# Two of a unit's four weight-block sums as accumulating transfers, and raw blocks loaded one by one

## The chip, the cores and the metric

The kernel runs on one core of one Trainium2 chip. The metric is device time in microseconds (us); a run's time is a little longer than the profile's span, which goes from the first to the last instruction. The engines are TensorE (PE: matmuls; PEld: its weight loads), VectorE (DVE), ScalarE (ACT), GpSimd (POOL) and SyncE (SP). SP and GpSimd issue nearly all DMA transfers, each in the order of its own queue.

## The reference

One layer of a hybrid decoder on 1024 prompt tokens and 8 decode tokens:

```
hn = rmsnorm(x, g_norm)
u  = hn @ w_in                       # 1024 -> 7176 columns
xa, za, q, k, v, o, zb, i, f = split(u)
yA = RG-LRU(conv(xa))                # a linear recurrence over the tokens
yB = rmsnorm(sigmoid(o) * mLSTM(q, k, v, i, f))
x  = x + concat[yA * silu(za), yB * silu(zb)] @ w_out
y  = rmsnorm(x, g_final)
```

The change lies in `hn @ w_in`, the input projection of the prompt tokens.

## The kernel before, in words

The wide columns of `w_in` are done in 14 units (`UNITS`, L44), each of two groups of 256 columns, such as `x0y0` (256 columns of xa, 256 of za). Unit 0 is done with plain products while the activations are read. Units 1 to 13 use Winograd's form of Strassen's scheme: a unit's weights are four blocks of 512 x 256, `blk(u, a, b)` with a the column group and b the half of the contraction (written A00, A01, A10, A11 for ab), the activations are cut in halves likewise, and seven products P1, P2, P5, P6, P7, P3, P4, in that order, stand in for eight. Fourteen operands of the activations (`cb`, high and low parts for seven products) are made once, in `x_combos` (L465).

Products are taken to fp32 accuracy by splitting each operand into a rounded high part and a low part (`split`, L70: ScalarE casts to `wh` on L72, VectorE subtracts to `wl` on L73) and three matmuls (`mm3`, L64, lines 66 to 68).

`prep(u, q)` (L276) makes the weight operand of product q. It forms four sums in place on VectorE, each over 128 x 1024 elements (L279, L280, L282, L288):

```
P5:  A00 = A00 - A10        L279
     A10 = A10 + A11        L280
P6:  A10 = A11 - A00        L282
     A01 = A01 - A10        L288, behind P6's split
```

and then splits A00 for P1, A01 for P2, A10 for P5, A10 for P6, A00 for P7, A01 for P3, A11 for P4. At P5, ahead of the sums, `dec_unit` (L251) multiplies all four raw blocks with the 8 decode tokens (L257). Raw blocks come from `w_in` through SP, 512 KB each (`load_raw`, L234 to L244), into two tiles: `raw0` with A00 and A10, `raw1` with A01 and A11. Both blocks of `raw0` are loaded for the next unit behind P7's split, both of `raw1` behind P4's.

`product(u, q)` (L299) runs the two halves s = 0 and 1 of a product, 24 matmuls of 512 columns in all (in v and o units 48 of 256). P1, P6, P7 and P4 add up in one accumulator (`ps_kv`), P2, P5 and P3 in another (`ps_o`), and `evac` (L325) takes a copy or a sum after each: ScalarE copies after P1, P5, P6 (L328, L335, L338) and P4 (L353), VectorE adds after P2, P7, P3 (L331, L341, L345). P6's copy on L338 must be done before P7 adds to the same accumulator. Outputs are stored by GpSimd's queue (`stq`).

The order of work is written out: the loop over `seq` (L1688) calls `preps`, which runs `LEAD` = 2 products ahead, then the product, and `pop_bg` after each half, which slips in one step of other work: gates, the RG-LRU (L772 are gate activations, L820 the gate products, L866 to L877 its stores), the decode step of the mLSTM (L988 to L1009). Each engine keeps its instructions in the order that the build lays out. Split operands live in six buffers (`NWS`, three products). The mLSTM over the prompt, the output projection and the final norm come after the units.

Of the kernel before, what the change touches and what calls it, by code (L numbers as in the profile page):

```python
# [17 lines left out]
P = 128  # L18
# [4 lines left out]
NH = 4  # L23
# [28 lines left out]
def hymba_kernel(  # L52
# [11 lines left out]
    def mm3(out, ah, al, bh, bl, first, last):  # L64

        TE.matmul(out, ah, bh, start=first, stop=False, skip_group_check=True)  # L66
        TE.matmul(out, ah, bl, start=False, stop=False, skip_group_check=True)  # L67
        TE.matmul(out, al, bh, start=False, stop=last, skip_group_check=True)  # L68

    def split(hi, lo, src):  # L70

        a = A.copy(hi, src)  # L72
        V.tensor_tensor(lo, src, hi.bitcast(F32), op=ALU.subtract)  # L73
        return a
# [7 lines left out]
    def ps(tag, shape):  # L82
        return psp.tile(shape, F32, tag=tag, name=f"ps_{tag}", bufs=NBUF.get(tag, 1))
# [139 lines left out]
    def run_late():  # L223
        now = late[:]
        late.clear()
        for f in now:
            f()
# [6 lines left out]
    def load_raw(u, b, parts=(0, 1)):  # L234

        if u >= len(units):
            return
        if (u, b) not in raws:
            raws[u, b] = rawp.tile([P, 4, 512], F32, tag=f"raw{b}", name=f"raw{b}_{u}")
        for a in parts:  # L240
            kind, j = units[u][a]
            c = COL[kind] + j * 256
            ld(raws[u, b][:, :, a * 256:(a + 1) * 256],
               w_in[0, b * HT:(b + 1) * HT, c:c + 256].rearrange("(k p) c -> p k c", p=P))  # L244
# [28 lines left out]
    def blk(u, a, b):  # L273
        return raws[u, b][:, :, a * 256:(a + 1) * 256]

    def prep(u, q):  # L276
        if q == Q_P5:
            dec_unit(u)
            V.tensor_tensor(blk(u, 0, 0), blk(u, 0, 0), blk(u, 1, 0), op=ALU.subtract)  # L279
            V.tensor_tensor(blk(u, 1, 0), blk(u, 1, 0), blk(u, 1, 1), op=ALU.add)  # L280
        if q == Q_P6:
            V.tensor_tensor(blk(u, 1, 0), blk(u, 1, 1), blk(u, 0, 0), op=ALU.subtract)  # L282
        src = {Q_P1: (0, 0), Q_P2: (0, 1), Q_P5: (1, 0), Q_P6: (1, 0), Q_P7: (0, 0), Q_P3: (0, 1), Q_P4: (1, 1)}
        hi, lo = ws([P, 4, 256], f"wh{u}_{q}"), ws([P, 4, 256], f"wl{u}_{q}")
        split(hi, lo, blk(u, *src[q]))
        wops[u, q] = hi, lo
        if q == Q_P6:
            V.tensor_tensor(blk(u, 0, 1), blk(u, 0, 1), blk(u, 1, 0), op=ALU.subtract)  # L288
        b = {Q_P7: 0, Q_P4: 1}.get(q)
        if b is not None:  # L290
            if u + 1 < len(units):
                load_raw(u + 1, b)
            else:
                if b == 1:
                    r_open(0)

    px = {}

    def product(u, q):  # L299

        kind = units[u][0][0]
        wh, wl = wops.pop((u, q))
        bh, bl = cb[q]
        first, last = q in (Q_P1, Q_P2, Q_P5), q in (Q_P2, Q_P3, Q_P4)
        for s in range(2):
            if q == Q_P1:
                px["X", s] = ps("kv", [P, 512])
            if q in (Q_P2, Q_P5):
                px["Y", s] = ps("o", [P, 512])
            X, Y = px["X", s], px.get(("Y", s))  # L310
            out = X if q in (Q_P1, Q_P6, Q_P7, Q_P4) else Y
            if kind in "vo":
                for i in range(2):
                    t = slice((2 * s + i) * P, (2 * s + i + 1) * P)
                    for k in range(4):
                        mm3(out[:, i * 256:(i + 1) * 256], bh[:, k, t], bl[:, k, t], wh[:, k, :], wl[:, k, :],
                            first and i == 0 and k == 0, last and i == 1 and k == 3)
            else:
                c = slice(s * P, (s + 1) * P)
                for k in range(4):  # L320
                    mm3(out, wh[:, k, c], wl[:, k, c], bh[:, k, :], bl[:, k, :], first and k == 0, last and k == 3)
            evac(u, q, s, X, Y)
            yield

    def evac(u, q, s, X, Y):  # L325
        if q == Q_P1:
            px["s1", s] = t = sg([P, 512], "s1")
            A.copy(t, X)  # L328
        elif q == Q_P2:
            t = px.pop(("s1", s))  # L330
            V.tensor_tensor(t, t, Y, op=ALU.add)  # L331
            emit_out(u, 0, 0, s, t)
        elif q == Q_P5:
            px["s5", s] = t = sg([P, 512], "s5")
            A.copy(t, Y)  # L335
        elif q == Q_P6:
            px["s2", s] = t = sg([P, 512], "s2")
            A.copy(t, X)  # L338
        elif q == Q_P7:
            t = px.pop(("s5", s))  # L340
            V.tensor_tensor(t, t, X, op=ALU.add)  # L341
            emit_out(u, 1, 1, s, t)
        elif q == Q_P3:
            t = px.pop(("s2", s))
            V.tensor_tensor(t, t, Y, op=ALU.add)  # L345
            emit_out(u, 0, 1, s, t)
        else:
            t = sg([P, 512], "c21")
            o = units[u][1][0] == "o"
            if o:  # L350
                A.activation(t, X, AF.Tanh, scale=0.5)
            else:
                A.copy(t, X)  # L353
            emit_out(u, 1, 0, s, t, o)

    def silu2(t):
# [108 lines left out]
    def x_combos(i):  # L465

        p0, p1 = xps[i]
        s = slice(i % 4 * P, (i % 4 + 1) * P)
        f0, f1 = bf["f"]

        def out(q, t):
            split(cb[q][0][:, :, s], cb[q][1][:, :, s], t)
        if i >= 4:
            t3 = sg([P, 4, P], "t3")
            V.tensor_tensor(t3, f1, f0, op=ALU.subtract)
            out(Q_P7, t3)
        else:
            t1, t2, t4 = (sg([P, 4, P], f"t{n}") for n in (1, 2, 4))
            V.tensor_tensor(t1, f0, p0, op=ALU.subtract)
            V.tensor_tensor(t2, f1, t1, op=ALU.subtract)  # L480
            V.tensor_tensor(t4, p1, t2, op=ALU.subtract)
            out(Q_P6, t2)
            out(Q_P5, t1)
            out(Q_P4, t4)
# [1191 lines left out]
    last_u = len(units) - 1  # L1676
    unit_of = {p: u for u, pair in enumerate(units) for p in pair}
    done_h = [max(unit_of[k, h] for k in "qkv") for h in range(NH)]

    def m_start():  # L1680
        state["m"] = True
        bg.append(m_open1)
        for n in range(NH):
            bg.extend(m_first(n))

    preps(LEAD)
    part = 0
    for n, (u, q) in enumerate(seq):  # L1688
        preps(n + 1 + LEAD)
        for _ in product(u, q):  # L1690
            pop_bg(2 if u == 1 or u == last_u else 1, 1, part % DEC[1 if u >= DEC[0] else 2] == 1)
            part += 1
        if u == last_u:
            wo_due(q)
        if q == 6:
            for kind, j in units[u]:
                if kind == "x":
                    rg_unit(j)
            for half in range(2):
                if u == max(unit_of["v", 2 * half], unit_of["v", 2 * half + 1], 1):  # L1700
                    bg.append(lambda half=half: dec_rows(half))
            for h in range(NH):
                if done_h[h] == u:
                    bg.append(lambda h=h: dcq.extend(decode_steps(h)))
            if u == last_u - 1:
                dgen = decode_outputs()

                def step():
                    next(dgen, None)
                    run_late()  # L1710
                state["out"] = [step] * 5 + [m_open2]
        if not state["m"] and u > max(done_h) and not (bg or rgq or dcq or late):
            m_start()
        if u == last_u and q == 0:
            if not state["m"]:
                while bg or rgq or dcq or late:
                    pop_bg()
                m_start()
            bg.extend(state["out"])
    while bg or late:  # L1720
        pop_bg()
    with tc.issue_after(lastt[0].ins):
# [102 lines left out]
```

## Time and profile before

| what | value |
|---|---|
| median of 3 runs | 915.24 us (914.72 to 915.32) |
| profiled execution's own time | 913.23 us |
| its span | 911.3 us |
| TensorE busy | 899.6 us |
| VectorE busy | 739.3 us |
| ScalarE busy | 585.0 us |
| GpSimd busy | 194.2 us |
| granted TensorE clock | 0.999 |

The profile page gives totals and the costliest groups: a line of the kernel, the engine, the operation, output <- inputs, how often, then busy time, the mean of one in ns, and the time that the engine stood idle just before. "Windows" give the busy time of each engine in a stretch; "waits" say who waited for whom, in total, how often, and at the longest; the timeline has the start, the length and the form of each instruction, with idle time ahead of it in brackets. Matmuls are pipelined, so their marked lengths overlap.

### The profile page before, as it was taken

What the parts mean: (1) busy time and instruction counts of PE and PEld (TensorE: products, weight loads), DVE (VectorE), ACT (ScalarE), POOL (GpSimd) and SP (SyncE); (2) the same over time, 40 slices, a digit from 0 to 9 for tenths busy, and PEclk for the clock granted to TensorE, in tenths of its full rate; (3) what the DMA queues carried; (4) which work ended last, traced back from release to release, by engine and by line L of the source; (5) the groups of instructions that cost most, each with busy time, mean ns of one, the idle gap of its engine ahead of it and who ended that gap; (6) DMA issues with size and microseconds to landing.
All of it is one profiled execution on the core that took longest, in us unless ns stands there. A gap on an engine that the chain in (4) does not pass through costs nothing. (4 is left out here: it accounts for less than half of the span.)

```text
span 911.3 us, 16738 instructions
## 1 busy us (share of the span) xinstructions
PE 899.6 (99%) x5889; PEld 762.3 (84%) x5889; DVE 739.3 (81%) x1528; ACT 585.0 (64%) x1086; POOL 194.2 (21%) x322
## 2 busy tenths in 40 slices
PE   8999999999999999999999999999999999999996
PEld 6997778877788997887789999887788888888886
DVE  6974778979698978789889876679998879888973
ACT  7653446867567776576658775446786568566642
POOL 1111112122222232324332334010111111121120
PEclk9999999999999999999999999999999999999999
DMA  6412447465746566548665747345679888855531
GB/s 200 149 64 92 139 147 250 135 205 187 236 128 221 171 203 204 197 145 266 201 237 184 253 139 244 108 133 191 215 234 259 202 216 296 217 142 180 181 124 67
DMA packets 130493, 167.76 MB, mean 184 GB/s; under 512 B 17596, under 2 KB 98564, under 8 KB 130402
## 3 DMA queue, kind: packets, MB, share of 16 engines
q1 hardware_dynamic: 108790, 103.68, 37.4%
q0 software_dynamic: 21616, 63.02, 20.9%
q8 instruction: 46, 0.75, 0.3%
q14 instruction: 37, 0.30, 0.1%
q10 hardware_dynamic: 4, 0.00, 0.0%
HBM read 108.00 MB, written 62.92 MB: 188 GB/s over the span
## 5 line engine op out<-in xcount | busy, mean ns | idle before, releaser
L72 ACT CAST wh<-raw 128x1024 fp32r<-128x1024 f32 x91 | 95.4, 1049 | 79.5 <-DVE raw L280 21.0
L73 DVE TENSOR_TENSOR wl<-raw,wh 128x1024 fp32r<-128x1024 f32 x91 | 111.1, 1221 | 29.4 <-ACT wh L72 15.8
L66 PE MATMUL ps_kv<-cb_hi,wh 128*128 128x512 f32 x320 | 127.4, 398 | 0.0
L68 PE MATMUL ps_kv<-cb_hi,wl 128*128 128x512 f32 x320 | 125.5, 392 | 0.0
L67 PE MATMUL ps_kv<-cb_lo,wh 128*128 128x512 f32 x320 | 125.2, 391 | 0.0
L66 PE MATMUL ps_o<-cb_hi,wh 128*128 128x512 f32 x240 | 95.2, 397 | 0.0
L68 PE MATMUL ps_o<-cb_hi,wl 128*128 128x512 f32 x240 | 93.7, 391 | 0.0
L67 PE MATMUL ps_o<-cb_lo,wh 128*128 128x512 f32 x240 | 93.6, 390 | 0.0
L66 PEld LDWEIGHTS ps_kv<-cb_hi,wh 128*128 128x128 f32 x320 | 60.1, 188 | 15.9 <-issue 3.1
L68 PEld LDWEIGHTS ps_kv<-cb_hi,wl 128*128 128x128 f32 x320 | 60.1, 188 | 13.4 <-issue 0.6
L67 PEld LDWEIGHTS ps_kv<-cb_lo,wh 128*128 128x128 f32 x320 | 60.1, 188 | 12.7 <-issue 0.8
L66 PE MATMUL ps_kv<-wh,cb_hi 128*128 128x256 f32 x192 | 55.1, 287 | 0.0
L67 PE MATMUL ps_kv<-wl,cb_hi 128*128 128x256 f32 x192 | 54.4, 283 | 0.0
L68 PE MATMUL ps_kv<-wh,cb_lo 128*128 128x256 f32 x192 | 54.3, 283 | 0.0
L66 PEld LDWEIGHTS ps_o<-cb_hi,wh 128*128 128x128 f32 x240 | 45.1, 188 | 10.4 <-issue 0.8
L68 PEld LDWEIGHTS ps_o<-cb_hi,wl 128*128 128x128 f32 x240 | 45.0, 188 | 9.9
L66 PE MATMUL ps_o<-wo,mh 128*128 128x512 f32 (+1 forms) x136 | 53.0, 390 | 0.0
L67 PEld LDWEIGHTS ps_o<-cb_lo,wh 128*128 128x128 f32 x240 | 45.1, 188 | 8.9
L68 PE MATMUL ps_o<-wo,ml 128*128 128x512 f32 (+1 forms) x136 | 51.6, 380 | 0.0
L67 PE MATMUL ps_o<-wo,mh 128*128 128x512 f32 (+1 forms) x136 | 51.5, 379 | 0.0
L66 PE MATMUL ps_o<-wh,cb_hi 128*128 128x256 f32 x144 | 41.0, 284 | 0.0
L67 PE MATMUL ps_o<-wl,cb_hi 128*128 128x256 f32 x144 | 40.7, 283 | 0.0
(559 smaller groups left out, 2603.8 us busy)
## 6 DMA issues: line engine op xcount, KB each, us to landing
raw<-in_w_in_dram SPq DMA_DIRECT2D x55, 512.0 KB
Cb<-in_state_mlstm_C_dram SPq DMA_DIRECT2D x32, 256.0 KB
out_dram<-Cb POOLq DMA_DIRECT2D x32, 256.0 KB, 4.9
qk<-d_qk SPq DMA_DIRECT2D x32, 256.0 KB
ring<-d_ro SPq DMA_DIRECT2D x26, 256.0 KB
d_qk<-s POOLq DMA_DIRECT2D x24, 256.0 KB, 4.8
d_x<-s POOLq DMA_DIRECT2D x16, 256.0 KB, 2.8
zsr<-d_y SPq DMA_DIRECT2D x16, 256.0 KB
```

What stands on the lines that cost most here:

```text
L66: TE.matmul(out, ah, bh, start=first, stop=False, skip_group_check=True)
L67: TE.matmul(out, ah, bl, start=False, stop=False, skip_group_check=True)
L68: TE.matmul(out, al, bh, start=False, stop=last, skip_group_check=True)
L72: a = A.copy(hi, src)
L73: V.tensor_tensor(lo, src, hi.bitcast(F32), op=ALU.subtract)
```

## The change

In units 1 to 12, two of the four sums become transfers from `w_in` that add to what stands in the raw tile (`accum_op=add`), issued by GpSimd. For that the signs are moved so that every sum is a plain one:

```
P5:  A10 = A10 + A11        VectorE
P6:  A10 = A10 + A00        VectorE
     A00 = A00 + A10 (w_in) transfer, for P7
     A10 = A10 + A01 (w_in) transfer behind P6's split, for P3
```

P3 now takes its operand from A10's place and not from A01's. The last unit keeps four sums on VectorE, in the new signs. The turned signs show in `x_combos` (t1, t2, t4) and `evac` (P7: -t - X; P4: -X, or tanh with scale -0.5 for o).

Each raw tile is now one tile for the whole run, and its blocks are loaded for the next unit one by one: A01 at P6, A00 at P7, A10 at P3, A11 at P4. The loop over `seq` becomes a loop over units and (product, half) pieces, with the calls in the same places as before.

```diff
+    def add(u, dst, src, here):
+        if here:
+            V.tensor_tensor(blk(u, *dst), blk(u, *dst), blk(u, *src), op=ALU.add)
+        else:
+            stq(blk(u, *dst), w_blk(u, *src), accum_op=ALU.add)
+
+    SRC = {Q_P1: (0, 0), Q_P2: (0, 1), Q_P5: (1, 0), Q_P6: (1, 0), Q_P7: (0, 0), Q_P3: (1, 0), Q_P4: (1, 1)}
+    FREED = {Q_P6: (0, 1), Q_P7: (0, 0), Q_P3: (1, 0), Q_P4: (1, 1)}
     def prep(u, q):
+        end = u == last_u
         if q == Q_P5:
             dec_unit(u)
-            V.tensor_tensor(blk(u, 0, 0), blk(u, 0, 0), blk(u, 1, 0), op=ALU.subtract)
-            V.tensor_tensor(blk(u, 1, 0), blk(u, 1, 0), blk(u, 1, 1), op=ALU.add)
+            if end:
+                add(u, (0, 0), (1, 0), True)
+            add(u, (1, 0), (1, 1), True)
         if q == Q_P6:
-            V.tensor_tensor(blk(u, 1, 0), blk(u, 1, 1), blk(u, 0, 0), op=ALU.subtract)
+            if end:
+                V.tensor_tensor(blk(u, 1, 0), blk(u, 1, 1), blk(u, 0, 0), op=ALU.add)
+            else:
+                add(u, (1, 0), (0, 0), True)
+                add(u, (0, 0), (1, 0), False)
...
         if q == Q_P6:
-            V.tensor_tensor(blk(u, 0, 1), blk(u, 0, 1), blk(u, 1, 0), op=ALU.subtract)
+            if end:
+                add(u, (0, 1), (1, 0), True)
             else:
-                if b == 1:
-                    r_open(0)
+                add(u, (1, 0), (0, 1), False)
+        if not end:
+            if q in FREED:
+                a, b = FREED[q]
+                load_raw(u + 1, b, (a,))
...
-            V.tensor_tensor(t, t, X, op=ALU.add)
+            V.scalar_tensor_tensor(t, t, -1.0, X, op0=ALU.mult, op1=ALU.subtract)
...
-                A.copy(t, X)
+                A.mul(t, X, -1.0)
```

More of the change, by code (lines that the diff above doesn't have):

```diff
@@ L284, in prep @@
         hi, lo = ws([P, 4, 256], f"wh{u}_{q}"), ws([P, 4, 256], f"wl{u}_{q}")
-        split(hi, lo, blk(u, *src[q]))
+        split(hi, lo, blk(u, *((0, 1) if q == Q_P3 and end else SRC[q])))
         wops[u, q] = hi, lo
         if q == Q_P6:
[L288 to L292, printed above, removed]
-            else:
-                if b == 1:
-                    r_open(0)
+            if end:
+                add(u, (0, 1), (1, 0), True)
+            else:
+                add(u, (1, 0), (0, 1), False)
@@ L297, in hymba_kernel, with product @@
+        if not end:
+            if q in FREED:
+                a, b = FREED[q]
+                load_raw(u + 1, b, (a,))
+        elif q == Q_P4:
+            r_open(0)
     px = {}
-    def product(u, q):
+    def product(u, q, s):
         kind = units[u][0][0]
-        wh, wl = wops.pop((u, q))
+        wh, wl = wops.pop((u, q)) if s == 1 else wops[u, q]
         bh, bl = cb[q]
         first, last = q in (Q_P1, Q_P2, Q_P5), q in (Q_P2, Q_P3, Q_P4)
[L305 to L319, printed above, removed]
-                for k in range(4):
-                    mm3(out, wh[:, k, c], wl[:, k, c], bh[:, k, :], bl[:, k, :], first and k == 0, last and k == 3)
-            evac(u, q, s, X, Y)
-            yield
@@ new lines, in product @@
+        if q == Q_P1:
+            px["X", s] = ps("kv", [P, 512])
+        if q in (Q_P2, Q_P5):
+            px["Y", s] = ps("o", [P, 512])
+        X, Y = px["X", s], px.get(("Y", s))
+        out = X if q in (Q_P1, Q_P6, Q_P7, Q_P4) else Y
+        if kind in "vo":
+            for i in range(2):
+                t = slice((2 * s + i) * P, (2 * s + i + 1) * P)
+                for k in range(4):
+                    mm3(out[:, i * 256:(i + 1) * 256], bh[:, k, t], bl[:, k, t], wh[:, k, :], wl[:, k, :],
+                        first and i == 0 and k == 0, last and i == 1 and k == 3)
+        else:
+            c = slice(s * P, (s + 1) * P)
+            for k in range(4):
+                mm3(out, wh[:, k, c], wl[:, k, c], bh[:, k, :], bl[:, k, :], first and k == 0, last and k == 3)
@@ L325, in evac @@
+        evac(u, q, s, X, Y)
     def evac(u, q, s, X, Y):
@@ L1684, in m_start @@
             bg.extend(m_first(n))
+    PIECES = [(q, s) for q in range(7) for s in range(2)]
+    PREP = range(0, 14, 2)
+    DUE = range(1, 14, 2)
     preps(LEAD)
     part = 0
-    for n, (u, q) in enumerate(seq):
-        preps(n + 1 + LEAD)
-        for _ in product(u, q):
+    for u in range(1, len(units)):
+        for n, (q, s) in enumerate(PIECES):
+            if n in PREP:
+                preps(7 * (u - 1) + PREP.index(n) + 1 + LEAD)
+            product(u, q, s)
             pop_bg(2 if u == 1 or u == last_u else 1, 1, part % DEC[1 if u >= DEC[0] else 2] == 1)
@@ L1692, in hymba_kernel @@
             part += 1
[L1693 to L1717, printed above, removed]
-                m_start()
-            bg.extend(state["out"])
+            if u == last_u and n in DUE:
+                wo_due(DUE.index(n))
+            if n == 13:
+                for kind, j in units[u]:
+                    if kind == "x":
+                        rg_unit(j)
+                for half in range(2):
+                    if u == max(unit_of["v", 2 * half], unit_of["v", 2 * half + 1], 1):
+                        bg.append(lambda half=half: dec_rows(half))
+                for h in range(NH):
+                    if done_h[h] == u:
+                        bg.append(lambda h=h: dcq.extend(decode_steps(h)))
+                if u == last_u - 1:
+                    dgen = decode_outputs()
+                    def step():
+                        next(dgen, None)
+                        run_late()
+                    state["out"] = [step] * 5 + [m_open2]
@@ L1720, in hymba_kernel @@
+            if n % 2 and not state["m"] and u > max(done_h) and not (bg or rgq or dcq or late):
+                m_start()
+            if u == last_u and n == 1:
+                if not state["m"]:
+                    while bg or rgq or dcq or late:
+                        pop_bg()
+                    m_start()
+                bg.extend(state["out"])
     while bg or late:
```

22 lines of the change are left out of this document (11 added, 11 removed).

## The prediction

> **What bounds the kernel now.** I read the page first, then the table of stages, then who waited for whom on TensorE, and last the order of time inside one unit.
>
> ```profile
> span 911.3 us, 16738 instructions
> PE 899.6 (99%) x5889; PEld 762.3 (84%) x5889; DVE 739.3 (81%) x1528; ACT 585.0 (64%) x1086; POOL 194.2 (21%) x322
> HBM read 108.00 MB, written 62.92 MB: 188 GB/s over the span
> ```
>
> TensorE (PE) is marked busy for all but 11.7 us of the span; VectorE (DVE), from which the change takes work, stands at 81%. The table of stages says where TensorE is idle. Its columns are the stretch, its length, then busy time and number of instructions of PE, PEld, DVE, ACT and POOL, the granted clock, and the DMA share. Units 1 to 13 run from 72.5 to 656.5 us; one of them (call it unit 8, an x/y unit) from 383.0 to 426.1.
>
> ```profile
> 383.00:426.10 43.10, 43.10 (x255) 34.85 (x251) 40.43 (x72) 30.40 (x44) 14.97 (x24) 1.00 0.56 181
> 656.50:911.30 254.80, 247.33 (x1430) 212.32 (x1428) 208.81 (x559) 159.87 (x424) 40.09 (x61) 1.00 0.67 192
> 72.50:656.50 584.00, 583.23 (x3912) 488.33 (x3911) 477.65 (x856) 378.78 (x566) 143.63 (x234) 1.00 0.57 187
> ```
>
> In 584.0 us of units TensorE is idle for 0.77 us; in the mLSTM stage behind them, which the change doesn't touch, for 7.5 us. The waits of that stretch add up to the same:
>
> ```profile
> PE ps_s L1069 <- DVE dworkb L1067: 0.4, 1, 0.4
> PE ps_tr L257 <- DMA raw<-in_w_in_dram: 0.3, 1, 0.3
> ```
>
> Neither is a wait for one of the four sums. But a busy mark isn't a peak, so I looked at the spacing of the matmuls.
>
> ```profile
> 406.11 0.39 PE L67 MATMUL ps_kv<-cb_lo,wh 128*128 128x512 f32 x1
> 406.33 0.39 PE L68 MATMUL ps_kv<-cb_hi,wl 128*128 128x512 f32 x1
> 406.56 0.39 PE L66 MATMUL ps_kv<-cb_hi,wh 128*128 128x512 f32 x1
> 412.00 0.39 PE L66 MATMUL ps_o<-cb_hi,wh 128*128 128x512 f32 x1
> L257 PE MATMUL ps_o<-raw,hnd 128*32 128x128 f32 x68 | 2.2, 274 | 0.0
> L1009 PE MATMUL ps_qp<-Cb,qfirst 128*32 128x256 f32 x8 | 0.6, 391 | 0.0
> L894 PE MATMUL ps_s<-dxs,graw 128*128 128x8 f32 x4 | 0.5, 235 | 0.0
> 383.00:426.10 43.10, 1.87 (x6) 1.13 (x6) 1.00 0.56 181
> ```
>
> Each lasts 0.39 us, but the next starts 0.22 to 0.23 us later (406.11, 406.33, 406.56): call it 0.226. (The matmul at 406.56 is the first of product P7, that at 412.00 the first of P3; the last row is the unit's stretch again for the gate products of L820 alone, six of them.) Unit 8 has 7 products of 24 such matmuls, 168 x 0.226 = 38.0 us. Of its other 87, the decode products of L257 take 2.2 us, L1009 0.6, L894 0.5, and the six gate products, which have the wide shape, 6 x 0.226 = 1.4. That makes 42.7 of 43.1 us, so at most 0.4 us of the unit can be a gap that busy marks hide. TensorE is full, and the change takes no matmul away.
>
> The Trainium skill ("Trainium Kernel Development and Optimization", section Best Practices) says that matmul busy time doesn't show the distance to the roofline, and to go by LDWEIGHTS busy instead. That agrees with 0.39 us marked for 0.226 us of spacing, and would let the 84% of PEld stand for room to speed up; it is the third rival below.
>
> **The change, part by part.** *Sums taken from VectorE.* The four sums of a unit are these groups, 13 of each:
>
> ```profile
> L288 DVE TENSOR_TENSOR raw<-raw,raw 128x1024 f32<-128x1024 f32 x13 | 15.9, 1221 | 0.4
> L279 DVE TENSOR_TENSOR raw<-raw 128x1024 f32<-128x1024 f32 x13 | 15.9, 1221 | 2.2 <-PE ps_tr L257 2.0
> L282 DVE TENSOR_TENSOR raw<-raw,raw 128x1024 f32<-128x1024 f32 x13 | 15.9, 1220 | 0.2
> L280 DVE TENSOR_TENSOR raw<-raw,raw 128x1024 f32<-128x1024 f32 x13 | 15.8, 1219 | 0.2
> ```
>
> In 12 units L279 and L288 go; the last unit keeps all four. VectorE loses 24 x 1.22 = 29.3 us (739 to 710). None of it ends a TensorE wait, so its worth on the path is 0, and at most the 0.77 us of idle time above. What it does is bring the chain of a unit forward: one sum, not two, before P5's cast, and no L288 ahead of P6's low part. Here is that chain in unit 8, DVE and ACT in order of time:
>
> ```profile
> 389.00 1.22 DVE L282 TENSOR_TENSOR raw<-raw,raw 128x1024 f32<-128x1024 f32 x1
> 394.66 1.05 ACT L72 CAST wh<-raw 128x1024 fp32r<-128x1024 f32 x1
> 395.00 1.22 DVE L73 TENSOR_TENSOR wl<-raw,wh 128x1024 fp32r<-128x1024 f32 x1
> 397.66 1.22 DVE L73 TENSOR_TENSOR wl<-raw,wh 128x1024 fp32r<-128x1024 f32 x1
> 400.14 1.05 ACT L72 CAST wh<-raw 128x1024 fp32r<-128x1024 f32 x1 [1.93 <-PE ps_o L67]
> 401.09 0.58 ACT L335 COPY s<-ps_o 128x512 f32<-128x512 f32 x1
> 401.56 0.69 ACT L772 ACTIVATE rg<-ps_s,hb 64x512 f32<-64x512 f32 x1
> 402.13 1.22 DVE L73 TENSOR_TENSOR wl<-raw,wh 128x1024 fp32r<-128x1024 f32 x1
> 403.54 0.58 ACT L338 COPY s<-ps_kv 128x512 f32<-128x512 f32 x1 [0.57 <-PE ps_kv L68]
> ```
>
> The cast at 394.66 is P7's, that at 400.14 P3's; the low parts at 395.00, 397.66 and 402.13 are P6's, P7's and P3's. P7 is split by 398.9 and first used at 406.56: 7.7 us of cover. P3 is split by 403.4 and used at 412.00: 8.6 us.
>
> *Accumulating transfers added.* Per unit two of 512 KB, issued by GpSimd. The first adds A10 to A00 and can go when the sum of L282's place is done; P7's cast waits for it. The second adds A01 into A10's place, after P6's split; P3's cast waits for it. No accumulation into on-chip memory of this size stands in the trace. The nearest are the 256 KB ones into d_p of L1435; for more bytes I take the software queue's own rate.
>
> ```profile
> L1435 POOL DMA_DIRECT2D d_p<-r x16: 836/850/949, 670.7 to 778.9; - x16
> DMA to landing us min/median/max: 4.0/5.5/9.9
> q0 software_dynamic: 21616, 63.02, 20.9%
> ```
>
> 63.02 MB in 20.9% of 16 x 911.3 us is 20.7 KB per us of one DMA engine, so another 256 KB on 16 engines, counted twice because an accumulation reads what it writes, takes 524 KB / (16 x 20.7) = 1.6 us. My estimate is 7.1 us from issue to landing, between 5.6 and 11.5, from L1435 as the only row that accumulates such an amount. In unit 8 the first is issued at 390.2 and lands at 397.3 (395.8 to 401.7); with cast and low part (1.05 + 1.22) P7 is split by 399.6 (at the latest 404.0), before 406.56. The second, after 396.2, lands at 403.3 (401.8 to 407.7) and P3 is split by 405.6 (at the latest 410.0), before 412.00. So the products' own operands are covered even at the upper bound; without the cover a unit would lose up to the transfer's 11.5 us. The Trainium skill ("DMA: Bandwidth & Descriptors", section Anatomy of one DMA) fits 2.0 us plus bytes over 436 GB/s, an estimate of 3.2 us for 512 KB; by it no cast would wait at all and the slower rival would fall away. L1435's 5.5 us for half as much speaks for the longer time.
>
> *Behind the new waits.* P3's cast, if it is held, holds ScalarE: behind it stand L335, two gate activations like that at 401.56, and L338, which reads P6's accumulator before P7 may add to it at 406.56. L338 must start by 406.56 - 0.58, so the cast by 406.0 - 1.05 - 0.58 - 2 x 0.69 = 403.0. The two sums gone from VectorE bring P6's low part up to 2.4 us forward, its end to 393.8, and the landing to 400.9: in time by 2.1 us, and it is late from a landing of 9.2 us on, by 2.3 us at 11.5. GpSimd's queue is the other danger: it runs in order, and in unit 8 it has a run of eight stores, the first and the last pair of them being
>
> ```profile
> 393.23 0.71 POOL L866 DMA_DIRECT2D d_ro<-rm  x1 [9.41 <-DVE rm L865]
> 398.04 1.12 POOL L368 DMA_DIRECT2D d_x<-s  x2
> ```
>
> Behind that run the second transfer is issued at 399.2 and lands at 406.3, 3.3 us after 403.0. Cost taken: 0, as the chain comes forward and the split ends close to the run's start; bounds: 0 to 3.3 us a unit, and no gain, since no wait goes with it. The queue waits first for VectorE, then for the split, and stores stand behind; 24 issues of about 0.85 us make 20 us on an engine at 21%. Memory reads grow by 24 x 0.524 = 12.6 MB from 108.0, and the DMA share of the units by 24 x 2 x 1.6 / 584 = 0.13, from 0.57 to 0.70.
>
> *Loads one by one; signs.* A01's load can go at P6, not after P4, the others after P7, P3 and P4.
>
> ```profile
> ACT wh L72 <- DMA raw<-in_w_in_dram: 12.5, 3, 4.5
> SPq L243 <- DVE wl L73: 80.0, 17, 22.8
> ```
>
> Only 3 casts ever waited for a raw block; the block that the next unit wants first, A00, is still loaded after P7, so nothing follows on the path: 0. SP's queue, which stood 80.0 us behind low parts of L73, gets one more such wait a unit, P3's, with the decode loads behind it. The turned signs keep the number of instructions; a scaled copy in L353's place or a scalar_tensor_tensor in L341's has its neighbours' length, in covered time: 0. The loop over (product, half) emits the same pieces in the same places.
>
> The sum: the profiled execution took 913.23 us, its span of 911.3 and 1.9 around it; minus 0, plus 0. It lies 2.0 us under the median of the runs (915.24; 914.72 to 915.32), so the same sum for a median is 915.2. About 0.2%, or 1.8 us, is what a measurement of this kernel can tell from no change.
>
> **Rivals.** *Held ScalarE (slower).* The second transfer lands later than 9.2 us after P6's split and P7 stalls behind L338, as worked out. For it: the 9.9 us among L1435's landings, DMA engines at 0.57 already, and GpSimd's run of stores. Against it: ScalarE is busy for 30.4 of 43.1 us in unit 8, and the built order may put the cast elsewhere. At 1.2 us, about the middle of 0 to 2.3, in half of the 12 units: 7 us, 922.
>
> *Late products (slower too, farther off).* A transfer outlasts the 7.7 us of cover with its two split steps: only above the upper bound. Each us past it costs a us in each of 12 units: 927.
>
> *Hidden gaps (faster).* By the skill's rule the 99% could hide time lost to VectorE. Rows give 0.4 us in unit 8, times 12 is 4.8, and with the idle 0.77 at most 5.6 us; half of it makes 912.4. Against it: the gaps sit wherever one kind of matmul follows another, with no VectorE wait beside them.
>
> *Not what it says.* The sums go, but a held GpSimd queue moves the same delay into stores and their buffers: with TensorE covered again, 915.2.
>
> **How the numbers follow.** No change 0.50 (forecast 0.47, the last rival 0.03); hidden gaps 0.20; held ScalarE 0.25 and late products 0.05, together slower 0.30. The range takes the faster case down to 912.0 and the slower one to 922.0, leaving out the largest gain and the second slower case.
>
> **What would show it.** Right: L279's and L288's successors only once in the profile, VectorE near 710 us, TensorE idle by about 1 us between 72.5 and 656.5, GpSimd near 214 us, landings of the new transfers at 5.6 to 11.5 us, casts of P7 or P3 waiting for them now and then while no matmul does. Wrong: TensorE idle or gaps by L66 behind L338 (held ScalarE), by wh or wl (late products), or a unit stage well under 584 us with the same matmuls (hidden gaps).

## The result, and the profile after

The changed kernel takes 940.87 us (median of 6 runs, 935.81 to 944.61), the kernel before beside it 915.53 (914.72 to 916.73). The ratio is 1.0268, 95% interval 1.0234 to 1.0302: 25 us slower. The forecast of no change (915.2) was wrong, and the time lies beyond the upper end of the range, 922.0. The profiled execution took 939.99 us.

These are the rows of the page of the changed kernel that answer to those of before, with the group of the new transfers and their row among the DMA issues.

```profile
span 938.2 us, 16802 instructions
PE 909.5 (97%) x5889; PEld 767.7 (82%) x5889; DVE 714.2 (76%) x1504; ACT 585.3 (62%) x1086; POOL 226.7 (24%) x346
HBM read 120.58 MB, written 62.92 MB: 196 GB/s over the span
L284 POOL DMA_DIRECT2D raw<-in_w_in_dram x24 | 31.7, 1343 | 67.5 <-PE ps_o L68 17.7
raw<-in_w_in_dram POOLq DMA_DIRECT2D x24, 512.0 KB, 7.4
```

VectorE did get lighter (739.3 to 714.2 us). The 24 transfers read the 12.6 MB that were worked out, and issuing one costs GpSimd 1.34 us. Now the stages: first the units, then all behind them.

```profile
72.30:683.40 611.10, 593.26 (x3914) 493.80 (x3911) 452.48 (x831) 379.16 (x566) 176.15 (x258) 0.99 0.70 199
683.40:938.20 254.80, 247.38 (x1430) 212.40 (x1428) 208.64 (x559) 159.78 (x424) 40.08 (x61) 0.99 0.67 192
```

The stage behind the units is as long as before (254.80). The units grew by 27.1 us, and TensorE, idle there for 0.77 us before, is idle for 611.10 - 593.26 = 17.8. The waits of TensorE that are new or longer than 1 us in this stage are these (line, what it waited for, us in total, times, longest).

```profile
PE ps_kv L66 <- ACT s L357: 12.3, 7, 4.0
PE ps_s L945 <- DVE OC L932: 2.5, 1, 2.5
PE ps_o L66 <- DVE s L350: 2.3, 1, 2.3
```

L357 is P6's copy (L338 before): P7 may not add to the accumulator until ScalarE has copied it. That is the wait that the slower rival named, in 12.3 of 17.1 us, but the units below show that ScalarE is late for different reasons. The loss by unit, from each unit's first matmul to the next one's, less the same of before, is 6.8 us in unit 2, 1.8 in 5, 3.6 in 6, 5.9 in 7, 4.4 in 8 and 4.5 in 11; the six others with transfers lose nothing, nor does unit 13.

**Unit 8** shows the rival's chain. First GpSimd's queue (start, length, line): the run of stores ends in the second transfer, at 415.51. Then ScalarE, with its idle time and what ended it in brackets, and TensorE.

```profile
412.68 1.42 POOL L896 DMA_DIRECT2D d_ro<-rt  x2
414.09 1.43 POOL L896 DMA_DIRECT2D d_ro<-r  x2
415.51 1.36 POOL L284 DMA_DIRECT2D raw<-in_w_in_dram  x1
...
423.15 1.05 ACT L72 CAST wh<-raw 128x1024 fp32r<-128x1024 f32 x1 [7.13 <-DMA raw<-in_w_in_dram]
424.11 0.58 ACT L354 COPY s<-ps_o 128x512 f32<-128x512 f32 x1
424.58 0.68 ACT L791 ACTIVATE rg<-ps_s,hb 64x512 f32<-64x512 f32 x1
425.29 0.68 ACT L791 ACTIVATE ig<-ps_s,hb 64x512 f32<-64x512 f32 x1
426.00 0.58 ACT L357 COPY s<-ps_kv 128x512 f32<-128x512 f32 x1
...
426.64 0.50 PE L66 MATMUL ps_kv<-cb_hi,wh 128*128 128x512 f32 x1 [2.12 <-ACT s L357]
```

P3's cast stands 7.13 us for its block, and behind it, in the forecast's order, come the copy of P5, two gate activations and P6's copy; P7's first matmul waits 2.12 us for that. The transfer needed some 7.6 us from its issue.

**The clock.** The stall is only half of what the unit lost. These windows of the changed kernel lie around unit 7's stall (the last two: unit 8's); the number ahead of the DMA share is the granted clock.

```profile
382.00:384.00 2.00, 1.48 (x6) 1.19 (x7) 1.92 (x2) 1.42 (x2) 0.00 (x0) 0.92 1.10 368
384.00:386.00 2.00, 2.00 (x6) 1.53 (x5) 1.98 (x5) 1.24 (x2) 0.93 (x2) 0.50 0.26 63
386.00:388.00 2.00, 2.00 (x8) 1.64 (x7) 2.00 (x5) 1.05 (x1) 2.00 (x4) 0.72 0.79 209
...
426.00:428.00 2.00, 1.36 (x6) 1.15 (x7) 0.00 (x0) 1.95 (x3) 0.00 (x0) 1.00 0.66 178
428.00:430.00 2.00, 2.00 (x7) 1.54 (x6) 1.90 (x3) 1.94 (x4) 0.00 (x0) 0.52 0.25 87
```

Some 1.2 and 1.5 us after matmuls begin again (382.5 and 426.6), the clock falls to a half: in unit 7, 0.92, 0.50 and 0.72 add up to 0.3 + 2.0 + 1.1 = 3.4 us at half speed, 1.7 us lost. The trace's clock record has five such stretches of 3.41 us in the units, at 148.2, 329.1, 383.7, 428.1 and 581.7 us, each beside a stall of 1.9 us or more: 5 x 1.7 = 8.5 us. With 17.1 us of new idle time that is 25.6 of the 27.1. The Trainium skill ("TensorE: Matmul & The Clock Gate", section What's actually happening) says that the clock is halved after an idle window of about 3.4 us and that the window runs freely. The 3.41 us at half clock agree with that length; that 3.4 idle us are needed doesn't, as four of the five stalls here were of 1.9 to 2.5 us.

**Unit 7** is another case: no cast waits. GpSimd's queue, with the decode step's value stores (L963, 8 KB each), then VectorE and ScalarE:

```profile
356.90 1.32 POOL L284 DMA_DIRECT2D raw<-in_w_in_dram  x1 [3.50 <-issue]
357.70 1.60 POOL L963 DMA_DIRECT2D d_dv<-vr  x2
...
368.18 0.88 DVE L1009 SCALAR_TENSOR_TENSOR Cb<-vbc,kw,Cb 128x256 f32<-128x256 f32 x2 [6.07 <-DMA vbc<-d_dv]
...
381.37 0.63 ACT L861 ACTIVATE na<-na 128x512 f32<-128x512 f32 x1 [6.37 <-DVE na L860]
381.90 0.57 ACT L357 COPY s<-ps_kv 128x512 f32<-128x512 f32 x1
```

From issue to landing, the four value stores (two here, two in unit 2) took in the changed kernel

```profile
DMA to landing us min/median/max: 5.2/6.2/7.0
```

and in the kernel before

```profile
DMA to landing us min/median/max: 1.6/1.8/2.9
```

Two small stores went out right behind the first transfer and landed late by some 4 us. The loads that read the values back (into the tile vbc) came late, VectorE stood 6.07 us, its RG-LRU step was late, and ScalarE stood 6.37 us for that, ahead of P6's copy. TensorE's longest wait (4.0 us) is the end of this chain.

**Unit 6** is a third. ScalarE's state step of the decode (L1007; L988 before), in the changed kernel and in the kernel before:

```profile
318.77 0.72 ACT L1007 ACTIVATE Cb<-Cb,dGI 128x512 f32<-128x512 f32 x1 [6.55 <-DMA Cb<-in_state_mlstm_C_dram]
327.38 0.59 ACT L357 COPY s<-ps_kv 128x512 f32<-128x512 f32 x1
```

```profile
306.16 0.72 ACT L988 ACTIVATE Cb<-Cb,dGI 128x512 f32<-128x512 f32 x1 [0.50 <-DMA Cb<-in_state_mlstm_C_dram]
```

The windows of 6 us from 11 us into the unit, in the same order (the DMA share is the last number but one):

```profile
312.00:318.00 6.00, 6.00 (x52) 6.00 (x51) 4.56 (x8) 0.22 (x1) 1.48 (x2) 1.00 1.17 232
```

```profile
304.00:310.00 6.00, 6.00 (x52) 6.00 (x51) 5.96 (x11) 5.42 (x7) 1.09 (x2) 1.00 0.41 135
```

SP issues the state's load 10.5 us into the unit in both. Before, the DMA engines are busy by 0.41 there and ScalarE waits 0.50 us; after, two transfers stand beside the load, the share is 1.17 (transfers overlap), and ScalarE waits 6.55. That the transfers make the load late is read from these rows.

**Units 11 and 2** fit none of these. In unit 11 ScalarE stands for vt, values that are read back from memory, ahead of the square root from which VectorE makes OC, the tile that TensorE waits for (2.5 us). No accumulating transfer is in this chain, and a kernel without transfers has it too (x10 below).

```profile
578.79 0.41 ACT L72 CAST vh<-vt 128x256 fp32r<-128x256 f32 x1 [3.38 <-DMA vt<-d_v]
```

Unit 2, the largest loss, has two stalls, one behind VectorE's sum on L350 (2.35 us, at 135.6) and one behind P6's copy (2.22 us, at 147.4), and one of the clock's stretches; its cause stays open.

So the theory after the result: ScalarE runs in order ahead of TensorE's copies, and the transfers make it late in three ways in units 5 to 8: by casts that wait for them (unit 8; unit 5 has such a cast too, with 1.97 us), by stores behind them in GpSimd's queue (unit 7) and by loads beside them (unit 6). The rivals: the casts alone; the load points; the bytes by themselves; or the rest of the change.

### The profile page after: what moved, and what is told of

It is laid out like the page before. It is cut to its first block, busy times and chain, and to the rows that moved or that the text cites. A ratio compares the mean times of both kernels' runs of the same rounds, so it can differ in the third digit from the quotient of the medians.

```text
span 938.2 us, 16802 instructions
## 1 busy us (share of the span) xinstructions
PE 909.5 (97%) x5889; PEld 767.7 (82%) x5889; DVE 714.2 (76%) x1504; ACT 585.3 (62%) x1086; POOL 226.7 (24%) x346
## 5 line engine op out<-in xcount | busy, mean ns | idle before, releaser
L66 PE MATMUL ps_kv<-cb_hi,wh 128*128 128x512 f32 x320 | 130.0, 406 | 10.1 <-ACT s L357 10.1
L68 PE MATMUL ps_kv<-cb_hi,wl 128*128 128x512 f32 x320 | 127.4, 398 | 0.0
L67 PE MATMUL ps_kv<-cb_lo,wh 128*128 128x512 f32 x320 | 127.1, 397 | 0.0
L284 POOL DMA_DIRECT2D raw<-in_w_in_dram x24 | 31.7, 1343 | 67.5 <-PE ps_o L68 17.7
L1007 ACT ACTIVATE Cb<-Cb,dGI 128x512 f32<-128x512 f32 x32 | 22.8, 721 | 33.2 <-DMA Cb<-in_state_mlstm_C_dram 30.8
```

The costliest lines, as they stand in the source:

```text
L284: stq(blk(u, *dst), w_blk(u, *src), accum_op=ALU.add)
L1007: A.mul(C, C, dGI[:, b, h:h + 1])
```

## The experiments

Ratios are to the kernel before on the same chip, with 95% intervals. The last columns are the loss of single units in us, from one profiled execution each; the changed kernel's own runs spread over 9 us, so single entries are rough. Of the units not shown, none loses more than 2.1 us (unit 10 in x3).

| kernel | us | ratio | 2 | 5 | 6 | 7 | 8 | 11 |
|---|---|---|---|---|---|---|---|---|
| changed | 940.87 | 1.0268 [1.0234, 1.0302] | 6.8 | 1.8 | 3.6 | 5.9 | 4.4 | 4.5 |
| x1 no transfers | 919.45 | 1.0052 [1.0037, 1.0067] | 2.7 | 0 | 0 | 0 | 0 | 2.0 |
| x6 no transfers, two load points | 920.11 | 1.0063 [1.0048, 1.0078] | 2.3 | 0 | 0 | 0 | 0 | 3.6 |
| x10 signs, tiles kept | 920.33 | 1.0050 [1.0031, 1.0070] | 2.3 | 0 | 0 | 0 | 0 | 4.0 |
| x11 signs alone | 915.13 | 0.9999 [0.9989, 1.0008] | 0.3 | 0 | 0 | 0 | 0 | 1.4 |
| x2 two load points | 938.39 | 1.0259 [1.0243, 1.0274] | 5.4 | 1.5 | 0.5 | 6.6 | 4.4 | 5.4 |
| x3 first transfer only | 929.81 | 1.0165 [1.0150, 1.0180] | 7.0 | 0.3 | 0 | 2.7 | 0 | 4.3 |
| x4 second only | 929.20 | 1.0152 [1.0135, 1.0169] | 6.3 | 1.4 | 0 | 0.1 | 4.6 | 4.2 |
| x8 six units | 919.54 | 1.0056 [1.0041, 1.0071] | 2.7 | 0 | 0 | 0.5 | 0 | 2.2 |
| x12 one fewer | 935.09 | 1.0219 [1.0200, 1.0238] | 3.6 | 1.7 | 2.1 | 8.3 | 0 | 5.6 |
| x5 traffic alone | 968.30 | 1.0585 [1.0548, 1.0622] | 2.8 | 0 | 0 | 0 | 0 | 5.8 |
| x9 traffic in place | 941.38 | 1.0278 [1.0258, 1.0299] | 11.5 | 0.3 | 6.6 | 6.1 | 0 | 1.7 |
| x7 value stores by SP | 933.31 | 1.0213 [1.0193, 1.0234] | 5.8 | 1.3 | 3.9 | 0.3 | 4.6 | 2.2 |
| x13 value and state stores by SP | 938.72 | 1.0258 [1.0235, 1.0282] | 6.4 | 0.9 | 0.5 | 3.8 | 2.8 | 7.2 |
| x14 splits later | 936.53 | 1.0231 [1.0214, 1.0248] | 4.8 | 1.8 | 4.0 | 6.2 | 4.3 | 7.3 |
| x15 x13 and x14 | 936.43 | 1.0240 [1.0206, 1.0274] | 7.5 | 0.7 | 0.8 | 3.9 | 2.6 | 5.7 |
| x16 x14 without transfers | 920.25 | 1.0058 [1.0043, 1.0073] | 2.9 | 0 | 0 | 0 | 0 | 2.6 |
| x17 casts tied | 931.07 | 1.0169 [1.0145, 1.0193] | 7.4 | 0 | 5.6 | 4.6 | 0.1 | 0 |
| x18 tied, value stores by SP | 924.74 | 1.0103 [1.0086, 1.0120] | 5.1 | 0 | 4.0 | 1.1 | 0 | 0 |

### Without the transfers, and by load points

x1: all four sums on VectorE, in the new signs.

```diff
-            if end:
+            if True:
                 add(u, (0, 0), (1, 0), True)
...
-                add(u, (1, 0), (0, 1), False)
+                add(u, (1, 0), (0, 1), True)
```

> All four sums on VectorE in the new signs, no accumulating transfer; raw tiles kept for the whole run and blocks loaded one by one at the same four points as in the changed kernel. Held casts (ScalarE waits at P7's or P3's cast for a transfer to land, and the copies behind it come late): 914 to 918 us, TensorE idle by about 1 us in units 1 to 13. Traffic (the added transfers make other transfers land later): also 914 to 918. Held loads (SP's queue stands longer at the raw loads, now four waits a unit, and the loads of the decode and RG-LRU work behind them come late): much of the loss stays, 925 to 935.

x2: the changed kernel with its loads at two points.

```diff
-    FREED = {Q_P6: (0, 1), Q_P7: (0, 0), Q_P3: (1, 0), Q_P4: (1, 1)}
+    FREED = {Q_P7: [(0, 0)], Q_P4: [(1, 0), (0, 1), (1, 1)]}
```

> The changed kernel with its transfers, but raw blocks loaded at two points of a unit as before: A00 behind P7's split, A10, A01 and A11 behind P4's. Held casts: no change against the changed kernel, 935 to 945 us. Traffic: the same, 935 to 945. Held loads: most of the 26 us comes back, 916 to 924.

x6 is x1 with x2's load points.

> As the run without transfers, but the raw blocks loaded at two points of a unit (A00 behind P7's split; A10, A01, A11 behind P4's). If the 4.6 us that stayed there come from the one-by-one loads: 914 to 916 us. If from the new signs or the raw tiles kept for the run: 918 to 921.

The transfers carry some 21 us: 940.87 to 919.45. The load points carry none, with transfers (938.39) or without (920.11). But 4.6 us stay when the transfers are gone, where the forecast had zero; x1 lies above the 914 to 918 that held casts and traffic gave. Two more kernels split this rest. x10 sums into A01 for P3 and loads in pairs, as before; x11 is x10 with a new raw tile for each unit:

```diff
-            raws[u, b] = raws[0, b] if (0, b) in raws else rawp.tile([P, 4, 512], F32, tag=f"raw{b}", name=f"raw{b}")
+            raws[u, b] = rawp.tile([P, 4, 512], F32, tag=f"raw{b}", name=f"raw{b}_{u}")
```

> No transfers; the four sums on VectorE in the places of the kernel before (A01 += A10 for P3), raw blocks loaded in pairs as before; what is left of the change is the new signs, the loop over pieces, and raw tiles kept for the whole run. If the 4.6 us that remained without transfers come from one of these three, 918 to 920 us. If they come from P3's operand standing in A10's place, 914 to 916.

> As the kernel with signs and kept tiles, but with a new raw tile for each unit, as before: new signs and the loop over pieces alone. If the kept tiles cost the 4.6 us, 914 to 916 us here and 918 to 920 there; if the signs or the loop cost them, 918 to 920 in both; if neither, 914 to 916 in both.

The signs and the new loop are free (915.13); keeping the tiles costs 5 us (920.33), in units 2 and 11. The tiles cover the same memory, but the built order of ScalarE differs: x10's has the cast of vt ahead of steps that x11's puts before it. Unit 11 of x11, then of x10 (which is 1.5 us behind there, by the cast ahead of these rows):

```profile
554.91 0.63 ACT L392 ACTIVATE s<-s 128x512 f32<-128x512 f32 x1 [1.71 <-DVE s L359]
...
556.85 0.26 ACT L924 ACTIVATE dxc<-dxc 128x64 f32<-128x64 f32 x1
...
561.37 0.41 ACT L72 CAST vh<-vt 128x256 fp32r<-128x256 f32 x1 [0.78 <-DMA vt<-d_v]
```

```profile
558.83 0.41 ACT L72 CAST vh<-vt 128x256 fp32r<-128x256 f32 x1 [4.09 <-DMA vt<-d_v]
...
560.55 0.26 ACT L925 ACTIVATE dxc<-dxc 128x64 f32<-128x64 f32 x1
...
562.12 0.63 ACT L393 ACTIVATE s<-s 128x512 f32<-128x512 f32 x1
```

ScalarE waits 4.09 us for vt instead of 0.78, the square root on L924 (L925), from which VectorE makes OC, comes 3.7 us later (2.2 beside the 1.5), and TensorE then waits 2.3 us for OC. With one stretch of half clock behind it (1.7 us, at 562.9) that is the 4.0 us of unit 11. That the order does it is read from these rows; no run changed this order alone, but x17 below keeps the tiles, has the other order in unit 11, and loses nothing there.

### Which transfer, and where

x3 has only the first transfer, x4 only the second. This is x3's edit:

```diff
-                add(u, (1, 0), (0, 1), False)
+                add(u, (1, 0), (0, 1), True)
```

> Only the first sum (A10 to A00, for P7) by transfer; the second on VectorE behind P6's split. Held casts: P7's cast has other work behind it before a copy that TensorE needs, so little is lost, 916 to 925 us. Traffic: half of the bytes, half of the loss, 926 to 930. Held loads: the four load points stay, 930 to 940.

> Only the second sum (A01 into A10's place, for P3) by transfer; the first on VectorE at P5. Held casts: P3's cast stands ahead of the copy of P6 that P7 needs, so most of the loss stays, 926 to 938 us. Traffic: half of the loss, 926 to 930. Held loads: 930 to 940.

Each costs about 10 us over x1, but in different units: unit 8's loss and most of unit 5's belong to the second transfer (4.6, 1.4), and of unit 7's 5.9 us 2.7 come with the first alone, 0.1 with the second; unit 6 loses with neither alone. x3's 929.81 lies in the range that the bytes gave, above that of held casts, and x4's 929.20 in both; the next run speaks against the bytes. x8 keeps the transfers in the six units that lost nothing:

```diff
+        here = u not in (1, 3, 4, 9, 10, 12)
-            if end:
+            if here:
...
-                add(u, (1, 0), (0, 1), False)
+                add(u, (1, 0), (0, 1), here)
```

> The transfers in six units alone, 1, 3, 4, 9, 10 and 12, which lost nothing in the changed kernel; the other units have all sums on VectorE. If the loss depends on what stands beside a transfer (held casts, or the queue): as without transfers, 918 to 922 us. If each transfer costs its share of bytes: half of the way to the changed kernel, 928 to 932.

Twelve transfers there cost nothing (919.54 against 919.45). These units were chosen because they had lost nothing, so this shows that the loss isn't shared out by bytes: it depends on what stands beside a transfer. x12 puts unit 8's second sum back on VectorE, and nothing else:

```diff
-                add(u, (1, 0), (0, 1), False)
+                add(u, (1, 0), (0, 1), u == 8)
```

> The changed kernel with one of its 24 transfers fewer: unit 8's second is a VectorE sum again. If a held cast costs unit 8 its time, that unit's 4.4 us go and the others stay: 935 to 938 us beside the 940.9 of the changed kernel. If the loss is shared out by bytes moved, 1/24 of some 21 us goes, 0.9: 940.

Unit 8's 4.4 us are gone, as the held cast says; 0.9 was the price by bytes. The median falls by 5.8, but that alone would prove little: other units moved too (unit 2 lost 3.6, unit 7 8.3), and the intervals of the two kernels touch.

### The traffic without the waits

x5 sends the 24 transfers to memory that nobody reads, with all sums on VectorE:

```diff
+            if not end:
+                stq(scr[0], w_blk(u, 1, 0), accum_op=ALU.add)
...
+                stq(scr[1], w_blk(u, 0, 1), accum_op=ALU.add)
```

> All four sums on VectorE; beside them the 24 accumulating transfers of 512 KB at the same places of the program, into a buffer in memory that nothing reads. So the transfers take their room in GpSimd's queue and on the DMA engines, but no cast waits for them. Held casts: as without transfers, 918 to 922 us. Traffic and queue (other stores and loads land later behind the transfers): most of the changed kernel's loss, 932 to 942.

It doesn't answer: with nothing to wait for, all 24 went out between 8.8 and 110 us, and the units began at 116.8 instead of 72.5. x9 holds each back with a one-column GpSimd copy of P6's sum, or of P6's low part:

```diff
+        g = G.tensor_copy(dep[n], after)
+        with tc.issue_after(g.ins):
+            stq(scr[n], w_blk(*src), accum_op=ALU.add)
```

> All four sums are on VectorE in the new signs, loads one by one. 24 accumulating transfers of 512 KB still go out, each at its unit's place in GpSimd's queue (behind a one-column copy that waits for P6's sum, or for P6's low part), but into memory that nothing reads, so no cast waits for one. If the loss is the casts that the transfers hold, this stands near the kernel without transfers: 919 to 922 us. If it is the queue and the traffic (stores and loads that land later because the transfers stand before them), most of the loss stays: 932 to 940. If both share it, as unit 7 (a held store) and unit 8 (a held cast) suggest, 925 to 930, with unit 7's loss still there and unit 8's gone.

I expected 925 to 930; it took 941.38, as long as the changed kernel, with no cast that waits for a transfer. So the traffic in its place is enough for a loss of this size, though not for the same loss: units 5 and 8 are free of it (0.3, 0), and units 2, 6 and 7 lose 24.2 of the 26.4 us. x9's longest wait of TensorE (L366 is P6's copy), and rows of ScalarE and VectorE ahead of it, in units 2 and 7:

```profile
PE ps_kv L66 <- ACT s L366: 15.5, 3, 6.7
```

```profile
150.94 0.72 ACT L1016 ACTIVATE Cb<-Cb,dGI 128x512 f32<-128x512 f32 x1 [6.17 <-DMA Cb<-in_state_mlstm_C_dram]
...
382.75 0.88 DVE L1018 SCALAR_TENSOR_TENSOR Cb<-vbc,kw,Cb 128x256 f32<-128x256 f32 x2 [5.95 <-DMA out_dram<-Cb]
```

Again ScalarE is held ahead of P6's copy, by the decode step's DMAs (in unit 7 by way of VectorE). In unit 6, which loses 6.6 us here, ScalarE waits 3.62 and 1.44 us for loads of the state, with no cast that waits for a transfer; that speaks for the reading of unit 6 above. x9's transfers write memory, not on-chip tiles, and land later (median 8.5 us against 7.4), so its size can't be carried over.

### Taking single waits away

x7 is the changed kernel with the four value stores issued by SP:

```diff
-            stq(d_dv[2 * half + h], vr[:, h * 256:(h + 1) * 256])
+            ld(d_dv[2 * half + h], vr[:, h * 256:(h + 1) * 256])
```

> The changed kernel with one edit: the four 8 KB stores into d_dv are issued by SP, not by GpSimd, so that they don't stand behind a transfer in the software queue. Queue: unit 7's 5.9 us go (its loads of vbc wait for such a store), 932 to 937 us. Held casts: 938 to 944, unit 7 as it was.

7.6 us come back by the medians (5.0 by the ratios), and unit 7's loss falls from 5.9 to 0.3. x13 moves the state's stores to SP too (`stq(s_C...` to `ld(s_C...`):

> The changed kernel with all stores of the decode step (values and new state) issued by SP and no longer behind the transfers in GpSimd's queue. If the stores behind the transfers carry the loss of units 2, 6, 7 and 11, 922 to 929 us; if held casts carry it outside unit 7, as with the value stores alone moved, 932 to 936; if SP's queue, held by these stores, delays its loads, above 940.

This failed: 938.72, worse than x7 and in none of the ranges. Unit 6's loss is nearly gone (0.5), though ScalarE still waits 4.95 us there for the state's load (6.55 in the changed kernel); but units 7 and 11 lose more than in x7: SP's loads now stand behind the stores, and VectorE's waits for the values are 11.3 us in all (5.5 in x7, 6.7 in the changed kernel). x14 lays the splits of P7 and P3 out one product later, x15 is x13 and x14 together, x16 is x14's edit in x1:

```diff
-                preps(7 * (u - 1) + PREP.index(n) + 1 + LEAD)
+                later = PREP.index(n) in (2, 3) and u < last_u
+                preps(7 * (u - 1) + PREP.index(n) + 1 + LEAD - later)
```

> The changed kernel with the splits of P7 and P3 laid out one product later, so that their casts stand behind P5's and P6's copies and can't hold these; the transfers are issued where they were. If held casts cost units 5, 6 and 8 (and part of 2) their time, that goes: 926 to 934 us, with unit 7's loss still there. If casts don't matter, 939 to 942. If the shorter cover (one product, 5.4 us, for the landing's rest, the cast and the low part) costs more than it saves, above 942, with matmuls that wait for wl or wh.

> Both edits, the decode step's stores by SP and the splits one product later. If the two mechanisms make up the loss, what stays is the order that the kept tiles bring: 917 to 922 us. If something third is at work, above 926.

> Control without transfers (all sums on VectorE, loads one by one, kept tiles), with the splits of P7 and P3 laid out one product later: shows what the later place costs or gains by itself, beside 919.5 us with the splits in their old place. 917 to 921 if the place is neutral.

x14 (936.53) and x15 (936.43) are as slow as the changed kernel, and x16 (920.25) as fast as x1, but x14 and x15 didn't test what they were meant to. The built order left P3's cast ahead of the copies, and in unit 8 of x14 it stood there as before:

```profile
421.80 1.05 ACT L72 CAST wh<-raw 128x1024 fp32r<-128x1024 f32 x1 [7.03 <-DMA raw<-in_w_in_dram]
422.75 0.58 ACT L354 COPY s<-ps_o 128x512 f32<-128x512 f32 x1
```

x17 therefore ties the casts of P7 and P3 behind the second copy of P5 and P6 (beside x14's edit); x18 is x17 with x7's stores:

```diff
+            with tc.issue_after(copied[u, Q_P5 if q == Q_P7 else Q_P6].ins):
+                A.copy(hi, blk(u, *SRC[q]))
+            V.tensor_tensor(lo, blk(u, *SRC[q]), hi.bitcast(F32), op=ALU.subtract)
```

> The changed kernel with the casts of P7 and P3 tied by an explicit order behind P5's and P6's second copy on ScalarE, so that a cast that waits for its transfer holds no copy. If held casts cost units 5, 6 and 8 their time (9.8 us in the profile of the changed kernel), that goes and unit 7's loss stays: 928 to 933 us. If the casts hardly matter, 938 to 942. If the shorter cover costs more, above 942, with matmuls that wait for wh or wl.

> The tied casts and the decode step's value stores issued by SP. If held casts and stores behind transfers make up units 5 to 8, units 5 to 8 lose nothing and units 2 and 11 stay: 920 to 927 us. If something third is at work in units 5 to 8, above 930.

Both times came out inside the ranges of held casts and held stores: 931.07 and 924.74. The units did so only in part. Units 5 and 8 lose nothing any more in x17, as held casts say. But unit 6, named with them, loses 5.6 us in x17 and 4.0 in x18, and unit 11, which was to stay, loses nothing; so the sizes fit partly by luck. ScalarE's waits for raw blocks in the changed kernel (30.4 of these 34.0 us are for transfers), and then in x17, where the tied casts have a line of their own, L306:

```profile
ACT wh L72 <- DMA raw<-in_w_in_dram: 34.0, 11, 7.1
```

```profile
ACT wh L72 <- DMA raw<-in_w_in_dram: 3.7, 1, 3.7
ACT wh L306 <- DMA raw<-in_w_in_dram: 0.7, 1, 0.7
PE ps_kv L68 <- DVE wl L307: 3.4, 2, 2.6
```

The casts no longer hold ScalarE. The last row is a new wait of TensorE, for the low parts that now come later: the shorter cover costs something (1.3 us in x18). Unit 11 is no proof of a held cast, as it lost 4.0 us in x10 without transfers. Tying the casts moved its order too, and the square root now stands ahead of the cast of vt:

```profile
573.50 0.26 ACT L934 ACTIVATE dxc<-dxc 128x64 f32<-128x64 f32 x1
...
577.64 0.40 ACT L72 CAST vh<-vt 128x256 fp32r<-128x256 f32 x1
```

The clock didn't fall in the units of x18 at all. A version faster than both kernels isn't among these, and none was to be expected: without a stall TensorE is full.

## Why the prediction was wrong

- *TensorE is full, so the freed VectorE time is worth nothing:* right. x8's twelve transfers took twelve sums from VectorE, and the units that had them are as long as before to 0.5 us; no kernel is faster.
- *The landing, 7.1 us, between 5.6 and 11.5:* right: 7.4, from 5.9 to 10.3. The estimate of 3.2 us by the fit of the Trainium skill ("DMA: Bandwidth & Descriptors", section Anatomy of one DMA) falls: none of the 24 landed in under 5.9 us. (Behind the run of stores a cast would have waited even with 3.2 us, from 400.1 to 402.4, but in time for the 403.0 of the forecast.) In unit 8 the example (issue behind the stores, a late L338) came out almost to the number, seen from the unit's start: issue at 16.2 us and landing at 23.3 in the forecast, 14.6 and about 22.2 in the trace.
- *"Cost taken: 0, as the chain comes forward and the split ends close to the run's start":* this is the step that failed. Instead of 0, TensorE waited 12.3 us for P6's copies alone, and six units lost 27 us in the profile. The rival beside it had the right chain for units 8 and 5 (4.4 and 1.8 us; x12 and x17), with 1.2 us a unit as its price. It had neither the stores behind a transfer (unit 7), nor the loads beside it (unit 6), nor a changed order (unit 11). That half of the units lose, as it said, is luck: they lose for different reasons. Tying the casts brought 9.8 us back (9.1 by the ratios), but only 6.2 of the profile's loss are held casts in units 5 and 8, and unit 11's 4.5 went as its order changed.
- *A stall costs its own length:* not said, but used in every price. Five of the stalls came with 1.7 us lost to half clock each: 8.5 us of 27.
- *GpSimd's queue, "stores stand behind":* the sentence was there, and no price followed; the last rival moved the delay into stores and took TensorE for covered. The value stores behind the first transfer cost 5 to 8 us (x7 7.6, or 5.0 by the ratios; x18 against x17 6.3). One issue took 1.34 us and not 0.85, so GpSimd stood at 226.7 us and not 214.
- *The DMA share of the units, 0.57 to 0.70:* right to the digit (0.70), partly by luck, as it is a mean over a stage that had become 27 us longer; and I drew nothing from the mean. In unit 6 it stood for 0.41 to 1.17 in the very 6 us in which a state load was due.
- *Loads one by one: "nothing follows on the path: 0":* the load points cost nothing, but the tiles kept for them do, 5 us (x10 against x11), and in unit 11 the built order shows how. The warning that the order may put a cast elsewhere stood only as a point against the rival.
- *Signs and loop, 0:* right (x11).

In sum: of 25.3 us, tying the casts took away 9.8 (940.87 to 931.07) and moving the value stores 6.3 (to 924.74); 5.3 more lie between that and the kernels without transfers (919.45), and 4.6 between those and before (914.8 beside x1); that is 26.0, with medians from several chips. What stays open: unit 2; how the 5.3, which lie in units 2, 6 and 7 (5.1, 4.0 and 1.1 lost in x18), split between late state loads and the built order; and whether the tiles' 5 us are the order alone.

## What to carry to other kernels

When one engine is full, work taken from another buys nothing, while every transfer put in its place is a new wait in someone's in-order queue: list, for each such wait, what stands behind it up to the next step that feeds the full engine, and price it where the schedule is tightest, not by a mean over stages. Look also at what stands behind the new transfer in its own queue and which loads are due beside it. A reuse of buffers that changes no instruction can still change the built order, so compare the order of the engines before reading a few us as hardware.

## What the runs showed of the hardware beyond that

- Beside stalls of TensorE of about 2 us and more the granted clock was 0.50 for 3.41 us, and beside longer ones at times for two or three times as long (6.83 us with a stall of 5.3 in x12; 10.24 us in and after a wait of 6.7 in x9). It isn't a sharp rule: the 2.35 us stall at 135.6 us in the changed kernel, one of 2.4 us in x18 and one of 2.6 us in x7 brought none.
- An accumulating transfer of 512 KB took GpSimd 1.34 us to issue and 5.9 to 10.3 us to land; stores of 8 KB issued right behind it landed after 5.2 to 7.0 us instead of 1.6 to 2.9.
